# Convolution and GELU issued inside the second seven-product call of a feed-forward kernel

## The chip, the cores and the metric

The kernel runs on one NeuronCore of a Trainium2 chip. The metric is the device time of one execution in microseconds (us), as the median of several runs. The core's engines are TensorE (PE: matrix products; PEld is its weight loading), VectorE (DVE), ScalarE (ACT), GpSimd (POOL) and SyncE (SP, which here only starts DMAs). Each works through its own queue in order and waits for the others by semaphores.

## The reference

One layer of a decoder on 2048 prompt tokens and 64 sample tokens (8 sequences of 8), model width 1024, in float32: an attention mixer and a linear-attention mixer, an output projection, and a feed-forward block. The change touches the feed-forward block alone:

```
def conv_ffn(xn, conv_buf, w_up, conv_w, conv_b, w_down):
    up = xn @ w_up                                  # (T, 2 * 2816)
    g, u = jnp.split(up, 2, axis=-1)
    gp = jnp.concatenate([conv_buf, g], axis=1)     # two rows of the past in front
    c = conv_b + sum(conv_w[j] * gp[:, j:j + T] for j in range(3))
    h = jax.nn.gelu(c, approximate=False) * u
    return h @ w_down, gp[:, T:]
```

So the gate half `g` goes through a causal convolution of three taps along the tokens and a GELU, and is multiplied by the up half `u`; the product goes through the down projection.

## The kernel before, in words

The program runs the mixers first (up to about 1250 us of the profile), then the feed-forward block. Columns of the 2816-wide inner dimension lie on partitions (22 column tiles of 128), tokens along the free dimension. The 2112 tokens are cut into four chunks of 528 (two halves of H = 264). In a chunk the column tiles go in pairs, and the pairs in groups of 4, 4, 4, 4, 2 and 4 tiles, that is 2, 2, 2, 2, 1 and 2 pairs. Float32 products are made from three products of rounded parts (high times high, high times low, low times high), for which weights and inputs are split into a high part on ACT (line 70) and a low part on DVE (line 73).

For one pair of column tiles, `ffn` does this:

- the *gate call*: `strassen(c, f, 0, ...)` makes the gate columns of both tiles for both token halves, a 2 by 2 block product in seven products instead of eight. Each product is 12 matmuls of 128x128 by 264 columns (line 1628) into a PSUM bank: `pfa`, `pfb`, `pfa` again, `pfe`, `pfd`, `pfe` again, `pfd` again, numbered i = 0 to 6. Behind each product stands one evacuation: i = 0 copies to `p1` (ACT, line 1617), i = 1 adds the first result `o11` (DVE, line 1615), i = 2 copies to `u2` (ACT, line 1619), i = 3 makes the sum `u4`, i = 4 the result `o22`, i = 5 `o12` and i = 6 `o21` (all DVE, line 1615). The second use of `pfe` and of `pfd` adds to what is in the bank, so product 5 waits until `u4` has been read off and product 6 until `o22` has. `p1`, `u2` and `u4` have one buffer each. In the trace the results of a gate call are written to tiles `gt`, those of an up call to `up`.
- in the first pair of a group, the *down projection* of the group before (`down`, matmuls on line 92, sums on line 1656) is emitted between the gate call and what follows.
- for each tile j of the pair, the convolution: tap 2 and the bias in one ACT activation (line 1689), the copy of the last two rows to `halo` (DVE, line 1690), taps 1 and 0 as two DVE instructions (line 1698), and the GELU (ACT, line 1704). In the last chunk, which has the sample tokens, small copies (lines 1694 to 1696) and two small tap instructions (line 1702) are added.
- the *up call*: `strassen(c, f, 1, ...)`, as the gate call.
- for each tile the product of both (line 1708) and its split into `hh` and `hl` (lines 70 and 73), the input of the down projection.

Inside each `strassen` call the weights come from `wsrc`. In chunk 0 (and for the first two pairs also in chunk 1) four sums make the combined weights (lines 1594 to 1597) and all seven are split; for later chunks four of the seven are loaded ready-made from DRAM (`ws<-d_wst`), and three are split. A ring of 8 slots holds split weights (`ws`), one of 4 raw weights (`wr`). After each product the call also takes one step of other work: of `pend` (normalisation of another chunk) after even products, of `xp` (`xprep`, which prepares the inputs of the next chunk; its stores are started from ACT's queue) after odd ones.

Instructions are emitted in the order of the Python code. The order in which each engine runs them is made when the program is built: a scheduler with its own model of durations goes through time and gives each engine an instruction that it takes to be ready, an earlier emitted one before a later one. `self.after(b, a)` adds an order between two instructions without a semaphore. So a place in the code is a priority, and `after` is a fixed order. Products of neighbouring calls are mixed on PE in this way.

Of the kernel before, what the change touches and what calls it, by code (L numbers as in the profile page):

```python
# [10 lines left out]
F32 = mybir.dt.float32  # L11
F32R = mybir.dt.float32r
I32 = mybir.dt.int32
AF = mybir.ActivationFunctionType
ALU = mybir.AluOpType
# [12 lines left out]
H = 264  # L28
# [8 lines left out]
class Layer:  # L37
# [1569 lines left out]
            if c == cs and 2 <= i < 6:  # L1607
                nc.sync.dma_start(wt[i - 2], t.bitcast(F32))

    def strassen(self, c, f, z, xs, pend, xp, o11, o12, o21, o22):  # L1610
        nc = self.nc
        ws = self.wsrc(c, f, z)
        pa, pb, pd, pe = (self.bank(n) for n in ("pfa", "pfb", "pfd", "pfe"))
        p1, u2, u4 = (self.spool.tile([128, H], F32, name=self.n(n), tag=n, bufs=b) for n, b in (("p1", 1), ("u2", 1), ("u4", 1)))
        add = lambda o, x, y: nc.vector.tensor_tensor(o, x, y[:, :H], op=ALU.add)  # L1615
        for i, (bank, new, ev) in enumerate((
                (pa, True, lambda: nc.scalar.copy(p1, pa[:, :H])),
                (pb, True, lambda: add(o11, p1, pb)),
                (pa, False, lambda: nc.scalar.copy(u2, pa[:, :H])),
                (pe, True, lambda: add(u4, u2, pe)),  # L1620
                (pd, True, lambda: add(o22, u4, pd)),
                (pe, False, lambda: add(o12, u2, pe)),
                (pd, False, lambda: add(o21, u2, pd)))):
            w = next(ws)
            for k in range(4):
                xh, xl = xs[self.PROD[i]][k]
                for j, (ww, xx) in enumerate(((0, xh), (0, xl), (1, xh))):
                    self.lastmm = nc.tensor.matmul(bank[:, :H], w[:, ww, k, :], xx, start=new and k == 0 and j == 0,  # L1628
                                                   stop=k == 3 and j == 2, skip_group_check=not new)
            ev()  # L1630
            if i % 2 == 0:
                pend and next(pend, None)
            else:
                next(xp, None)
        next(ws, None)
# [7 lines left out]
    def down(self, c, gi, f0, G, hs, acc, last):  # L1643
        nc = self.nc
        for m in range(KT):
# [14 lines left out]
                self.ssq_add(self.fssq, acc[m], 2 * H, m == 0)  # L1660
            yield

    def ffn(self, c, xs, pend, more=None):
        nc, a, p, sp = self.nc, self.a, self.npool, self.spool
        halo, sc = self.halo, self.sc
        t0 = FCH[c][0]
        w = 2 * H
        npr = min(w, S - t0)
        acc = []
        f = 0  # L1670
        down = None
        xp = self.xprep(c + 1) if c < 3 else iter(())
        for gi, G in enumerate(FG):
            hs = []
            for pi in range(G // 2):
                gts = [self.ftile("gt", 3) for _ in range(2)]
                for j in range(2):
                    nc.vector.tensor_copy(gts[j][:, 0:2], halo[:, f + j, :])
                self.strassen(c, f, 0, xs, pend, xp if gi else iter(()), *(gts[j][:, 2 + z * H:2 + z * H + H] for j in range(2) for z in range(2)))
                if down is not None:  # L1680
                    for _ in down:
                        pass
                    down = None
                cts = []
                for j in range(2):
                    gt, ff = gts[j], f + j
                    ct = self.ftile("ct", 3)
                    cts.append(ct)
                    nc.scalar.activation(ct, gt[:, 2:], AF.Identity, bias=self.cw[:, ff, 3:4], scale=self.cw[:, ff, 2:3])
                    nc.vector.tensor_copy(halo[:, ff, :], gt[:, npr:npr + 2])  # L1690
                    gs = None
                    if npr < w:
                        gs = sp.tile([128, 8, 10], F32, name=self.n("gs"), tag="gs", bufs=2)
                        nc.vector.tensor_copy(gs[:, :, 0:2], sc[:, ff])
                        nc.vector.tensor_copy(gs[:, :, 2:10], gt[:, 2 + npr:].rearrange("p (b t) -> p b t", b=8))
                        nc.vector.tensor_copy(self.co[:, ff], gs[:, :, 8:10])
                    for tap in (1, 0):
                        nc.vector.scalar_tensor_tensor(ct[:, :npr], gt[:, tap:tap + npr], self.cw[:, ff, tap:tap + 1],
                                                       ct[:, :npr], op0=ALU.mult, op1=ALU.add)
                        if gs is not None:  # L1700
                            cs = ct[:, npr:w].rearrange("p (b t) -> p b t", b=8)
                            nc.vector.scalar_tensor_tensor(cs, gs[:, :, tap:tap + 8], self.cw[:, ff, tap:tap + 1],
                                                           cs, op0=ALU.mult, op1=ALU.add)
                    nc.scalar.activation(ct, ct, AF.Gelu)
                ups = [self.ftile("up", 2) for _ in range(2)]
                self.strassen(c, f, 1, xs, pend, xp if gi else iter(()), *(ups[j][:, z * H:z * H + H] for j in range(2) for z in range(2)))
                for j in range(2):
                    nc.vector.tensor_tensor(cts[j], cts[j], ups[j], op=ALU.mult)
                    hi = self.t528("hh", "hhl", 8, F32R)
                    lo = self.t528("hl", "hhl", 8, F32R)  # L1710
                    self.split(hi, lo, cts[j], "v")
                    hs.append((hi, lo))
                f += 2
            last = gi == len(FG) - 1
            if (last or gi == (c == 0)) and pend is not None:
                for _ in pend:
                    pass
                pend, more = more, None
            if not (last and c == 3):
                down = self.down(c, gi, f - G, G, hs, acc, last)  # L1720
        if c == 3:
            nc.sync.dma_start(a["o_cp"], halo)
            nc.sync.dma_start(a["o_cs"], self.co)
            return self.ffn_end(c, acc, hs, f - G, G)
        for _ in xp:
            pass
        for _ in self.xload(c + 1):
            pass
        for _ in down:
            pass  # L1730
        return self.final(c, acc, self.fssq, 0, w)
# [324 lines left out]
```

## Time and profile before

| | |
|---|---|
| time, median of 3 runs | 2740.87 us (2739.98 to 2741.07) |
| the profiled execution: time, span | 2739.73 us, 2737.9 us |
| PE, DVE, ACT, POOL busy | 97%, 67%, 46%, 14% of the span |
| feed-forward matmuls on line 1628, first and last start | 1252.1 us, 2697.2 us |
| the four taps' group (line 1698) | 176 instructions, median 759 ns |
| tap 2 with bias (line 1689), GELU (line 1704) | 88 of each, median 816 ns and 645 ns |
| first result of the up call (`up<-p,pfb`, line 1615) | 44 instructions, median 421 ns |

The profile is that of one execution. Times of a row count from the start of the span. An engine's busy time is the time in which one of its instructions ran; in a row of the timeline, brackets hold how long the engine had been idle before and which instruction released it. `pfd L92 <- ACT ws L70` reads: instructions on line 92 that write `pfd` waited for ACT's instruction on line 70 that writes `ws`.

### The profile page before, as it was taken

The page shows a single profiled execution, that of the slowest core. Times are in us where ns is not written, and L with a number is a line of the kernel's source. Part 1 is how long each engine was busy: PE and PEld are TensorE (multiplying, and loading weights), DVE is VectorE, ACT ScalarE, POOL GpSimd, SP SyncE. Part 2 cuts the span into 40 slices and gives each one's busy share as a digit, 9 for nine tenths or more (in the row PEclk, how much of TensorE's full clock was granted, in tenths as well). Part 3 has the DMA queues.
Part 4 walks back from the last instruction along what each step waited for, and adds up shares of the span by engine and source line. Part 5 has one row for each costly group of instructions (what it writes and reads, how often), then busy time and mean ns, then how long its engine had stood idle before and what let it go on. Part 6 is the DMA issues. An engine that isn't in the chain of part 4 may idle for free. (4 is left out here: it accounts for less than half of the span.)

```text
span 2737.9 us, 58183 instructions
## 1 busy us (share of the span) xinstructions
PE 2658.4 (97%) x22203; PEld 2518.3 (92%) x22203; DVE 1845.9 (67%) x4441; ACT 1271.2 (46%) x2961; POOL 386.4 (14%) x540
## 2 busy tenths in 40 slices
PE   8999999999999998999999999999999999999997
PEld 6788899888788888998999999999999999999997
DVE  7645655555467775568898889765676765766666
ACT  6535433333378784445554445433344432443332
POOL 2223120000035773011000020000110000200001
PEclk9999999999999999999999999999999999999998
DMA  8755546799776662476787588886798766976654
GB/s 322 250 176 178 183 149 196 283 331 365 267 262 181 200 168 93 154 264 230 259 281 275 191 330 306 329 305 201 246 335 287 280 227 215 327 248 215 216 193 147
DMA packets 287015, 661.66 MB, mean 242 GB/s; under 512 B 32961, under 2 KB 82753, under 8 KB 284689
## 3 DMA queue, kind: packets, MB, share of 16 engines
q1 hardware_dynamic: 256528, 579.53, 61.3%
q0 software_dynamic: 13216, 46.56, 5.0%
q10 hardware_dynamic: 16992, 31.86, 3.1%
q8 instruction: 175, 2.87, 0.4%
q14 instruction: 104, 0.84, 0.1%
HBM read 511.45 MB, written 146.37 MB: 240 GB/s over the span
## 5 line engine op out<-in xcount | busy, mean ns | idle before, releaser
L70 ACT ACTIVATE ws<-wr 128x512 fp32r<-128x512 f32 (+1 forms) x482 | 292.9, 616 | 426.8 <-PE pfe L1628 133.6
L92 PE MATMUL pfd<-hh,ws 128*128 128x264 f32 x2816 | 476.7, 286 | 6.0 <-ACT ws L70 4.5
L92 PEld LDWEIGHTS pfd<-hh,ws 128*128 128x128 f32 x2816 | 402.1, 190 | 8.6 <-ACT ws L70 6.4
L73 DVE TENSOR_TENSOR ws<-wr,ws 128x512 fp32r<-128x512 f32 (+1 forms) x482 | 319.2, 668 | 123.7 <-ACT ws L70 118.9
L92 PE MATMUL pfd<-hl,ws 128*128 128x264 f32 x1408 | 303.1, 286 | 1.9 <-DVE hl L73 1.9
L1628 PE MATMUL pfe<-xh,ws 128*128 128x264 f32 x1496 | 291.4, 287 | 11.4 <-DVE u L1615 6.9
L1628 PE MATMUL pfa<-xh,ws 128*128 128x264 f32 x1496 | 289.9, 285 | 4.6 <-ACT ws L70 2.2
L1628 PE MATMUL pfd<-xh,ws 128*128 128x264 f32 x1408 | 289.6, 285 | 1.9 <-DVE up L1615 1.4
L1628 PEld LDWEIGHTS pfe<-xh,ws 128*128 128x128 f32 x1496 | 237.4, 190 | 13.1 <-DVE u L1615 7.8
L1628 PEld LDWEIGHTS pfa<-xh,ws 128*128 128x128 f32 x1496 | 235.0, 188 | 6.1 <-ACT ws L70 2.8
L399 PE MATMUL pv<-wh,xh 128*128 128x256 f32 (+1 forms) x816 | 233.9, 287 | 2.2 <-DVE th L696 2.2
L1628 PEld LDWEIGHTS pfd<-xh,ws 128*128 128x128 f32 x1408 | 231.4, 189 | 2.9 <-DVE up L1615 1.8
L399 PE MATMUL pv<-wl,xh 128*128 128x256 f32 (+1 forms) x816 | 232.1, 284 | 0.0
L399 PE MATMUL pv<-wh,xl 128*128 128x256 f32 (+1 forms) x816 | 232.0, 284 | 0.0
L92 PEld LDWEIGHTS pfd<-hl,ws 128*128 128x128 f32 x1408 | 226.6, 190 | 2.2 <-DVE hl L73 2.1
L1869 ACT ACTIVATE ass<-ass,aml 128x256 f32<-128x256 f32 (+1 forms) x384 | 173.5, 454 | 62.6 <-DVE aml L1865 61.4
L1628 PE MATMUL pfd<-xl,ws 128*128 128x264 f32 x704 | 200.7, 285 | 0.5 <-DMA xl<-d_xst 0.5
L92 PE MATMUL pq<-xh,wh 128*128 128x512 f32 (+2 forms) x480 | 173.0, 366 | 8.3 <-ACT xh L234 7.9
L1656 DVE TENSOR_TENSOR acc<-acc,pfd 128x264 f32<-128x264 f32 x304 | 116.3, 422 | 89.6 <-PE pfd L92 89.1
L1628 PE MATMUL pfe<-xl,ws 128*128 128x264 f32 x616 | 176.3, 286 | 0.0
L1628 PE MATMUL pfa<-xl,ws 128*128 128x264 f32 x616 | 174.8, 284 | 0.0
L92 PE MATMUL pq<-xh,wl 128*128 128x512 f32 (+2 forms) x480 | 173.0, 361 | 0.0
(332 smaller groups left out, 6286.4 us busy)
## 6 DMA issues: line engine op xcount, KB each, us to landing
ws<-d_wst SPq DMA_DIRECT2D x248, 512.0 KB, 5.3
wr<-in_wu SPq DMA_DIRECT2D x114, 512.0 KB, 4.7
d_wst<-ws SPq DMA_DIRECT2D x88, 512.0 KB, 3.4
wr<-in_wd SPq DMA_DIRECT2D x160, 256.0 KB, 3.9
wr<-in_wt SPq DMA_DIRECT2D x60, 512.0 KB, 8.1
wh<-d_wbs SPq DMA_DIRECT2D x35, 512.0 KB, 5.7
wl<-d_wbs SPq DMA_DIRECT2D x35, 512.0 KB, 5.3
skp<-in_ckt SPq DMA_DIRECT2D x16, 1024.0 KB, 7.6
```

Source lines behind the costliest of these rows:

```text
L70: h = nc.scalar.activation(hi, src, AF.Copy)
L73: return h, (nc.gpsimd if lo_eng == "p" else nc.vector).tensor_tensor(lo, src, hi.bitcast(F32), op=ALU.subtract)
L92: mm = nc.tensor.matmul(o, ww[:, k, :], xx[:, s0:s0 + n], start=(k == order[0] and i == 0), stop=(k == order[-1] and i == 2))
L399: mm = nc.tensor.matmul(ps[:m, :256], x[:, t0:t0 + m], w[:, k % 4, :], start=(k == 0 and i == 0), stop=(k == KT - 1 and i == 2))
L1628: self.lastmm = nc.tensor.matmul(bank[:, :H], w[:, ww, k, :], xx, start=new and k == 0 and j == 0, stop=k == 3 and j == 2, skip_group_chec ...
L1656: nc.vector.tensor_tensor(acc[m][:, s0:s0 + n], acc[m][:, s0:s0 + n], pz, op=ALU.add)
L1869: ex = nc.scalar.activation(ssb[:, sc:sc + nk], ssb[:, sc:sc + nk], AF.Exp, bias=self.ml[:, idx, h:h + 1], scale=-1.0, accum_out=self.ml[: ...
```

## The change

`strassen` takes a generator `mid` and goes one step of it on after each of its products; it also keeps each evacuation instruction in `self.lev[i]`. The convolution of a pair, which was emitted in front of the up call, becomes a generator `conv` that the up call is given as `mid`. Its five steps fall behind products 0 to 4 of the up call: tile 0's tap 2, bias and halo copy; tile 0's taps 1 and 0; tile 1's tap 2, bias and halo copy; tile 1's taps 1 and 0; both GELUs. In addition `after` orders tile 0's taps behind the up call's `o11` sum, tile 1's taps behind its `u4` sum (both on DVE), and both GELUs behind its `u2` copy (ACT). Both `ct` tiles of a pair are allocated before the call. No instruction is added or taken out.

```
-    def strassen(self, c, f, z, xs, pend, xp, o11, o12, o21, o22):
+    def strassen(self, c, f, z, xs, pend, xp, o11, o12, o21, o22, mid=None):
...
-            ev()
+            self.lev[i] = ev()
+            mid and next(mid, None)
             if i % 2 == 0:
                 pend and next(pend, None)
...
+    lev = {}
+
+    def conv(self, f, npr, gts, cts):
+        nc, w, halo = self.nc, 2 * H, self.halo
+        for j in range(2):
+            gt, ct, ff = gts[j], cts[j], f + j
+            nc.scalar.activation(ct, gt[:, 2:], AF.Identity, bias=self.cw[:, ff, 3:4], scale=self.cw[:, ff, 2:3])
+            nc.vector.tensor_copy(halo[:, ff, :], gt[:, npr:npr + 2])
...
+            yield
+            for tap in (1, 0):
+                st = nc.vector.scalar_tensor_tensor(ct[:, :npr], gt[:, tap:tap + npr], self.cw[:, ff, tap:tap + 1],
+                                               ct[:, :npr], op0=ALU.mult, op1=ALU.add)
+                self.after(st, self.lev[2 * j + 1])
...
+            yield
+        for ct in cts:
+            self.after(nc.scalar.activation(ct, ct, AF.Gelu), self.lev[2])
+        yield
...
-                cts = []
-                for j in range(2):
...
-                    nc.scalar.activation(ct, ct, AF.Gelu)
+                cts = [self.ftile("ct", 3) for _ in range(2)]
+                mid = self.conv(f, npr, gts, cts)
                 ups = [self.ftile("up", 2) for _ in range(2)]
-                self.strassen(c, f, 1, xs, pend, xp if gi else iter(()), *(ups[j][:, z * H:z * H + H] for j in range(2) for z in range(2)))
+                self.strassen(c, f, 1, xs, pend, xp if gi else iter(()), *(ups[j][:, z * H:z * H + H] for j in range(2) for z in range(2)), mid=mid)
+                for _ in mid:
+                    pass
```

More of the change, by code (lines that the diff above doesn't have):

```diff
@@ L1661, in down @@
             yield
+    lev = {}
[5 more added lines that the diff above has]
+            nc.vector.tensor_copy(halo[:, ff, :], gt[:, npr:npr + 2])
+            gs = None
+            if npr < w:
+                gs = self.spool.tile([128, 8, 10], F32, name=self.n("gs"), tag="gs", bufs=2)
+                nc.vector.tensor_copy(gs[:, :, 0:2], self.sc[:, ff])
+                nc.vector.tensor_copy(gs[:, :, 2:10], gt[:, 2 + npr:].rearrange("p (b t) -> p b t", b=8))
+                nc.vector.tensor_copy(self.co[:, ff], gs[:, :, 8:10])
+            yield
[3 more added lines that the diff above has]
+                self.after(st, self.lev[2 * j + 1])
+                if gs is not None:
+                    cs = ct[:, npr:w].rearrange("p (b t) -> p b t", b=8)
+                    nc.vector.scalar_tensor_tensor(cs, gs[:, :, tap:tap + 8], self.cw[:, ff, tap:tap + 1],
+                                                   cs, op0=ALU.mult, op1=ALU.add)
+            yield
+        for ct in cts:
+            self.after(nc.scalar.activation(ct, ct, AF.Gelu), self.lev[2])
+        yield
     def ffn(self, c, xs, pend, more=None):
@@ L1683, in ffn @@
                     down = None
-                cts = []
-                for j in range(2):
[L1686 to L1704, printed above, removed]
+                cts = [self.ftile("ct", 3) for _ in range(2)]
+                mid = self.conv(f, npr, gts, cts)
                 ups = [self.ftile("up", 2) for _ in range(2)]
-                self.strassen(c, f, 1, xs, pend, xp if gi else iter(()), *(ups[j][:, z * H:z * H + H] for j in range(2) for z in range(2)))
+                self.strassen(c, f, 1, xs, pend, xp if gi else iter(()), *(ups[j][:, z * H:z * H + H] for j in range(2) for z in range(2)), mid=mid)
+                for _ in mid:
+                    pass
                 for j in range(2):
```

## The prediction

> **What bounds the kernel now.** I read the page first (busy shares), then the feed-forward stage by chunk, then what the matrix engine (PE) waits for in each chunk, then the instructions around the largest wait in order of time.
>
> ```profile
> span 2737.9 us, 58183 instructions
> PE 2658.4 (97%) x22203; PEld 2518.3 (92%) x22203; DVE 1845.9 (67%) x4441; ACT 1271.2 (46%) x2961; POOL 386.4 (14%) x540
> ```
>
> PE is busy 97% of the span, so a change of work on DVE (VectorE) or ACT (ScalarE) can pay only where PE waits. The next view cuts the feed-forward stage into its four token chunks: columns are the length of the stretch, busy time of each engine (with its count of instructions), granted clock, DMA share and GB/s.
>
> ```profile
> core 0: us, PE busy (x) PEld busy (x) DVE busy (x) ACT busy (x) POOL busy (x), PEclk, DMA share, GB/s
> 1252.00:1630.00 378.00, 363.59 (x2924) 360.17 (x2924) 328.89 (x660) 196.00 (x360) 21.05 (x37) 0.99 0.71 255
> 1630.00:2002.00 372.00, 362.50 (x2937) 360.44 (x2936) 271.15 (x555) 154.33 (x288) 18.78 (x30) 0.99 0.80 282
> 2002.00:2359.00 357.00, 355.73 (x2919) 355.06 (x2918) 239.73 (x498) 141.29 (x264) 16.52 (x29) 1.00 0.77 271
> 2359.00:2700.00 341.00, 339.95 (x2783) 338.92 (x2781) 218.99 (x541) 128.28 (x240) 1.20 (x1) 1.00 0.69 231
> ```
>
> Chunks 2 and 3 leave PE idle 1.3 and 1.1 us in 357 and 341 us: nothing is to be had there, only lost. Chunk 0 leaves 14.4 us and chunk 1 leaves 9.5 us, and in chunk 0 DVE is busy 329 of 378 us. So the change is decided in chunks 0 and 1. What PE waited for there (us in total, times, longest), from the waits of chunk 0, then of chunk 1, then of chunks 2 and 3:
>
> ```profile
> PE pfe L1628 <- DVE u L1615: 6.9, 3, 5.6
> PE pfd L92 <- ACT ws L70: 3.4, 3, 2.0
> ...
> PE pfe L1628 <- DMA ws<-d_wst: 3.9, 3, 1.5
> PE pfd L92 <- DVE hl L73: 1.9, 1, 1.9
> PE pfa L1628 <- ACT ws L70: 1.2, 1, 1.2
> ...
> PE pfa L1628 <- ACT p L1617: 1.0, 2, 0.5
> ```
>
> The largest is one wait of 5.6 us for the sum `u4` (tile `u`). Around it, in order of time (start, duration, engine, line, out<-in, and in brackets the idle time before it): PE, then DVE, then ACT, then the stretch right behind the wait.
>
> ```profile
> 1271.79 0.28 PE L1628 MATMUL pfd<-xh,ws 128*128 128x264 f32 x1
> 1277.71 0.59 PE L1628 MATMUL pfe<-xh,ws 128*128 128x264 f32 x1 [5.64 <-DVE u L1615]
> ...
> 1270.58 0.76 DVE L1698 SCALAR_TENSOR_TENSOR ct<-gt,c_cw,ct 128x528 f32<-128x528 f32 x1
> 1271.25 0.68 DVE L1597 TENSOR_TENSOR wt<-wr,wt 128x512 f32<-128x512 f32 x1
> ...
> 1274.34 0.42 DVE L1615 TENSOR_TENSOR gt<-u,pfd 128x264 f32<-128x264 f32 x1
> ...
> 1275.95 0.68 DVE L1595 TENSOR_TENSOR wr<-wr 128x512 f32<-128x512 f32 x1
> 1276.56 0.76 DVE L1698 SCALAR_TENSOR_TENSOR ct<-gt,c_cw,ct 128x528 f32<-128x528 f32 x1
> 1277.23 0.42 DVE L1615 TENSOR_TENSOR u<-u,pfe 128x264 f32<-128x264 f32 x1
> ...
> 1274.79 0.83 ACT L1689 ACTIVATE ct<-gt,c_cw 128x528 f32<-128x528 f32 x1
> 1275.53 0.36 ACT L1619 COPY u<-pfa 128x264 f32<-128x264 f32 x1
> ...
> 1277.70:1282.20 4.50, 4.49 (x20) 4.50 (x21) 3.67 (x8) 1.52 (x3) 0.00 (x0) 0.50 0.07 27
> ```
>
> The tile `u2` has one buffer, so the copy `u2` (1275.53) of the up call could not be written before the gate call's last sum `gt<-u,pfd` (1274.34) had read the old one. ACT then did the tap-2 activation (L1689) first, because it is emitted earlier and was freed by the same sum; DVE did a weight sum and one tap (1276.56) before `u4`. PE lost 5.64 us, and then 4.5 us at a granted clock of 0.50, which costs 2.2 us more.
>
> **The change, part by part.** *No work is added or removed.* Per pair the moved step issues two L1689 activations, two halo copies, four taps (L1698; in chunk 3 also six small copies and four small taps) and two GELUs: all on DVE and ACT, no DMA, nothing on POOL or SP. It is moved behind the up call's weight loads on SP and behind the steps of the post chain and of `xprep` only in the order of emission; SP's queue holds none of its instructions. The work itself is therefore 0 us; what counts is place.
>
> *The pins.* Taps of tile 0 now stand on DVE behind the up call's first sum (`up<-p,pfb`), taps of tile 1 behind `u4`, GELUs on ACT behind `u2`. They are orders on one engine, so they add no semaphore; what queues behind a waiting tap is the next sums and the low halves of the weight splits, and behind a waiting GELU the high halves. That such waits happen is in the waits of ACT:
>
> ```profile
> ACT ct L1704 <- DVE ct L1698: 47.3, 34, 3.9
> ```
>
> That is 34 waits of a GELU for its tap; in chunks 2 and 3 they can have cost PE no more than the 1 us above. GELUs can't become late for their reader (L1708), which needs the call's last sum.
>
> *Gain 1: the 5.64 us wait.* `u2` is now emitted ahead of tile 1's L1689: it saves that activation's slot, 1275.53 - 1274.79 = 0.74 us. The tap at 1276.56 can't stand ahead of `u4` any more: 1277.23 - 1276.56 = 0.67 us, of which the weight sum at 1275.95 keeps a little. I take 1.3 us together. The two taps of tile 0 (one of them at 1270.58) may stay where they are, as their pin is already met, and so may the weight sums; hence `gt<-u,pfd` stays near 1274.34 and some 4.3 us of the wait stay, with the half clock behind it. Next late is the sum after `u4`. Bounds: 0, and the whole 5.6 + 2.2 = 7.8 us if the new order on DVE serves `gt<-u,pfd` at once.
>
> *Gain 2: second pair of chunk 1.* Rows of ACT, then PE, then the stretch behind them:
>
> ```profile
> 1671.65 0.83 ACT L1689 ACTIVATE ct<-gt,c_cw 128x528 f32<-128x528 f32 x1 [0.84 <-DVE gt L1615]
> ...
> 1673.05 0.39 PE L1628 MATMUL pfa<-xh,ws 128*128 128x264 f32 x1 [1.25 <-ACT ws L70]
> 1675.94 0.52 PE L1628 MATMUL pfa<-xh,ws 128*128 128x264 f32 x2 [0.94 <-DVE ws L73]
> ...
> 1678.50:1681.30 2.80, 2.78 (x12) 2.78 (x13) 2.49 (x7) 0.96 (x4) 0.00 (x0) 0.50 1.05 406
> ```
>
> The L1689 activation waited 0.84 us at the head of ACT's queue with a weight split behind it, and PE waited 1.25 us for that split. Emitted behind the up call's first product, it no longer stands ahead of that product's split. Bounds 0 and 1.25 + 0.94 = 2.2 us; I take the middle, 1.1 us. The last row shows a clock of 0.50 for 2.8 us behind these gaps, none of them longer than 1.25 us in the rows; so a half clock can outlive a long wait that is broken into short ones, and I count no gain for it here.
>
> On this the Trainium skill, "TensorE: Matmul & The Clock Gate", section "HAM oscillation — how this bites in real kernels", has the rule "no PE-idle gaps >~3.4µs". By that rule the 2.2 us behind the first wait would go as soon as less than 3.4 us of it were left; the row at 1678.50 does not agree that a single gap must be so long. With some 4.3 us left, both leave it in place.
>
> *Loss: the taps leave the down projection.* In every group but a chunk's first, the down projection of the group before runs between the first pair's gate and up calls. DVE used it for that pair's taps. First and last of the four taps of chunk 0's third pair, the sum behind which they must now stand, then the stretches by time: the down projection, and the five stretches from such an up call to the next down projection or group.
>
> ```profile
> 1320.22 0.76 DVE L1698 SCALAR_TENSOR_TENSOR ct<-gt,c_cw,ct 128x528 f32<-128x528 f32 x1
> ...
> 1325.94 0.76 DVE L1698 SCALAR_TENSOR_TENSOR ct<-gt,c_cw,ct 128x528 f32<-128x528 f32 x1
> ...
> 1345.58 0.41 DVE L1615 TENSOR_TENSOR up<-p,pfb 128x264 f32<-128x264 f32 x1
> ...
> 1313.00:1341.00 28.00, 28.00 (x231) 28.00 (x231) 19.25 (x37) 15.69 (x37) 0.00 (x0) 1.00 0.62 220
> 1341.00:1378.00 37.00, 36.39 (x296) 35.97 (x295) 35.05 (x69) 20.63 (x39) 0.00 (x0) 1.00 0.85 315
> ...
> 1406.00:1448.00 42.00, 38.63 (x309) 37.58 (x307) 39.03 (x78) 21.83 (x41) 0.00 (x0) 1.00 0.91 328
> ...
> 1476.00:1515.00 39.00, 39.00 (x322) 39.00 (x322) 34.39 (x68) 21.40 (x39) 0.00 (x0) 1.00 0.77 275
> ...
> 1542.00:1577.00 35.00, 35.00 (x290) 35.00 (x289) 27.55 (x61) 17.62 (x35) 0.00 (x0) 1.00 0.50 177
> 1577.00:1612.00 35.00, 33.26 (x268) 32.48 (x267) 30.75 (x63) 17.13 (x32) 9.68 (x18) 1.00 0.96 347
> ```
>
> The taps go some 20 us later, out of a stretch with 8.75 us of idle DVE into one with 1.95 us. A tap takes 0.67 us of DVE's queue (1270.58 to 1271.25), four take 2.7 us. The five stretches have 1.95, 2.97, 4.6, 7.5 and 4.3 us free. The first is short by 0.75 us; in the second PE already waits 3.4 us, so I charge half of the 2.7 us, 1.35; the others fit. Loss 2.1 us; bounds 0 and five times 2.7 = 13.6 us. In chunks 2 and 3 the same move finds room: in the up call of such a pair (chunk 3) DVE was idle ahead of `u4` and of the next split for
>
> ```profile
> 2443.90 0.43 DVE L1615 TENSOR_TENSOR u<-u,pfe 128x264 f32<-128x264 f32 x1 [2.81 <-ACT u L1619]
> ...
> 2447.40 0.69 DVE L73 TENSOR_TENSOR ws<-wr,ws 128x512 fp32r<-128x512 f32 x1 [2.01 <-ACT ws L70]
> ```
>
> 2.81 and 2.01 us, against 1.4 us of taps at each place (2.0 with chunk 3's small ones): 0. If that cover were gone, the ten such pairs of chunks 2 and 3 would pay up to 2.7 us each.
>
> *Sum.* -1.3 - 1.1 + 2.1 = -0.3 us. The profiled execution took 2739.73 us, of which the span is 2737.9; that is 1.1 us under the median of 2740.87. -0.3 on the median gives 2740.6 us. A measurement of this kernel tells some 0.2%, 5.5 us, from no change.
>
> **The rivals.** *B, the first wait goes whole.* For it: 2.3 us of DVE's queue stood between the end of PE's last product (1271.79 + 0.28 = 1272.07) and `gt<-u,pfd` at 1274.34, and moved priorities may dissolve it. Against it: most are weight work, which the move does not put later. It gives -7.8 - 1.1 and no loss: 2740.9 - 8.9 = 2732 us, or 2734 if the half clock outlives the wait. (The Trainium skill's rule on the clock gate, above, would have the first of these, the row at 1678.50 allows the second.)
>
> *C, slower: the pile in chunk 0.* Taps pinned behind `u4` stand ahead of the sum that frees the bank for the seventh product; where DVE is later than one product, PE stops. For it: 35.05 of 37 us busy, and PE waits already in two of the five stretches. Against it: free DVE in three of them. It decides once taps cost more than the free time: 2.7 us in the first two stretches and half of it in three is 9.5 us, less the 2.4 gained: 2748 us. All five in full: 2752.
>
> *D, nothing moves that PE sees.* Both gains and the loss are hidden behind fillers from the next call: 2740.9, inside the forecast.
>
> **How the numbers follow.** Forecast with D (gain and loss of like size): 0.52, its own range 2736 to 2745. B and lesser forms of it beyond 5.5 us: 0.26. C: 0.22. The range goes from 2731, just under B, to 2750, above C's 2748, and leaves out the full pile. So faster 0.26, same 0.52, slower 0.22.
>
> **What would show it.** Right: the wait for `u` in chunk 0 is 4 to 5 us with clock 0.50 behind it; PE idle in chunks 2 and 3 stays near 1 us; DVE idle in 1313 to 1341 grows by 2.7 us and shrinks after 1341. Wrong: the 5.6 us wait gone (B), new PE waits for `up` or `ws` after 1341 (C), or new waits in chunks 2 and 3, for which I have charged nothing.

## The result and the profile after

The change made the kernel faster: 2726.28 us (median of four runs, 2723.55 to 2730.01) against 2740.76 us, ratio 0.9947 [0.9933, 0.9961]. Repeated beside twelve runs of the kernel before it gave 2726.73 against 2736.69 us, ratio 0.9968 [0.9957, 0.9980]. In the later comparisons the kernel before had medians of 2735.4 to 2736.8 us over 116 runs (2730.3 to 2747.3), so the first four of it were among its slower ones, and I take the effect as some 10 us. In microseconds below, differences are differences of medians of runs made together.

The page after, of a run of 2730.01 us, 9.7 us less than the profiled run before; then the four chunks as in the prediction (length, PE busy, PEld, DVE, ACT, POOL, granted clock, DMA share, GB/s):

```profile
span 2728.2 us, 58216 instructions
PE 2657.1 (97%) x22203; PEld 2519.3 (92%) x22203; DVE 1852.7 (68%) x4441; ACT 1270.3 (47%) x2961; POOL 385.0 (14%) x540
```

```profile
1254.00:1629.00 375.00, 361.89 (x2924) 358.57 (x2924) 328.75 (x660) 196.89 (x360) 21.60 (x38) 0.99 0.72 256
1629.00:1992.00 363.00, 359.35 (x2937) 357.67 (x2937) 271.84 (x554) 153.46 (x288) 18.18 (x30) 1.00 0.82 291
1992.00:2352.00 360.00, 357.33 (x2922) 356.90 (x2921) 241.15 (x498) 141.06 (x264) 16.51 (x29) 1.00 0.77 268
2352.00:2690.00 338.00, 337.53 (x2771) 337.32 (x2770) 223.81 (x541) 127.35 (x240) 1.20 (x1) 1.00 0.68 233
```

The work is the same (x4441 on DVE, x2961 on ACT before and after). PE idle went from 14.4 to 13.1 us in chunk 0, from 9.5 to 3.7 in chunk 1, from 1.3 to 2.7 in chunk 2 and from 1.1 to 0.5 in chunk 3. That is 6.3 us. Time at half clock counts as busy: by the traces' clock records it cost PE 7.1 us before, in four stretches (near 1278, 1450, 1679 and 1696), and 4.0 us after, in two (near 1279 and 2171), which is 3.1 us less. By the starts of the chunks' first products in the trace (for chunk 3, to the start of its last product) the four took 378.2, 372.0, 357.3 and 337.6 us before and 375.3, 362.8, 359.9 and 335.3 us after. Together that is 11.7 us less, of which idle time and half clock are 9.4; the span gained only 9.7, as the first product started 2.0 us later.

The waits of PE after, in the order of the prediction (total, times, longest): chunk 0, chunk 1, chunks 2 and 3.

```profile
PE pfe L1628 <- DVE u L1615: 5.2, 3, 4.8
PE pfd L92 <- ACT ws L70: 3.2, 4, 1.2
PE pfa L1628 <- ACT ws L70: 2.8, 4, 1.0
...
PE pfe L1628 <- DMA ws<-d_wst: 0.9, 2, 0.5
PE pfa L1628 <- ACT ws L70: 0.7, 1, 0.7
...
PE pfa L1628 <- ACT p L1617: 3.1, 3, 2.2
```

The large wait of chunk 0 is still there, a little shorter. In chunk 1 the wait for `hl` (1.9 us) is gone. Chunk 2 has a new wait of 2.2 us for the copy `p`, with a half clock behind it. Around the large wait (PE, ACT, DVE, then the stretch behind it; in the changed kernel taps are L1680, the tap-2 activation L1670, the GELU L1689):

```profile
1278.84 0.59 PE L1628 MATMUL pfe<-xh,ws 128*128 128x264 f32 x1 [4.81 <-DVE u L1615]
...
1276.60 0.38 ACT L1619 COPY u<-pfa 128x264 f32<-128x264 f32 x1 [1.91 <-DVE gt L1615]
1276.88 0.83 ACT L1670 ACTIVATE ct<-gt,c_cw 128x528 f32<-128x528 f32 x1
...
1274.27 0.76 DVE L1680 SCALAR_TENSOR_TENSOR ct<-gt,c_cw,ct 128x528 f32<-128x528 f32 x1
...
1276.15 0.42 DVE L1615 TENSOR_TENSOR gt<-u,pfd 128x264 f32<-128x264 f32 x1
1278.37 0.41 DVE L1615 TENSOR_TENSOR u<-u,pfe 128x264 f32<-128x264 f32 x1
...
1278.90:1283.40 4.50, 4.50 (x20) 4.50 (x21) 4.28 (x9) 2.27 (x5) 0.00 (x0) 0.50 0.20 80
```

The copy `u2` now stands ahead of tile 1's tap-2 activation. But the sum `gt<-u,pfd`, for which it waits, is as late as before: taps of tile 0 and weight sums still stand in front of it. The half clock behind the wait stayed. What went is seen in chunk 1, where the prediction's second gain lies. Before, a third wait followed the two near 1673 and 1676 that the prediction shows (first row); after, two short ones are left:

```profile
1678.52 0.59 PE L1628 MATMUL pfe<-xh,ws 128*128 128x264 f32 x1 [1.10 <-DMA ws<-d_wst]
...
1670.69 0.39 PE L1628 MATMUL pfa<-xh,ws 128*128 128x264 f32 x1 [0.72 <-ACT ws L70]
1673.27 0.52 PE L1628 MATMUL pfa<-xh,ws 128*128 128x264 f32 x2 [0.62 <-DVE ws L73]
```

Three waits of 3.3 us in all became 1.3 us, and the half clock there (1.7 us) went with them: the granted clock was 1.00 from 1670 to 1685.

### The profile page after: what moved, and what is told of

It is laid out like the page before. It is cut to its first block, busy times and chain, and to the rows that moved or that the text cites. A ratio compares the mean times of both kernels' runs of the same rounds, so it can differ in the third digit from the quotient of the medians.

```text
span 2728.2 us, 58216 instructions
## 1 busy us (share of the span) xinstructions
PE 2657.1 (97%) x22203; PEld 2519.3 (92%) x22203; DVE 1852.7 (68%) x4441; ACT 1270.3 (47%) x2961; POOL 385.0 (14%) x540
## 4 chain that ended last, share of the span: by engine, by line
PE 77%; DMA 8%; DVE 7%; POOL 3%; issue 3%; ACT 2%; SPq 0%; DVEq 0%; POOLq 0%; ACTq 0%
PE pfd L92 16%; PE pv L399 9%; PE pfe L1628 8%; PE pfd L1628 8%; PE pq L92 8%; PE pfa L1628 8%; PE pbo L1431 7%; PE pfb L1628 4%; PE pas L1872 2%; DMA raw<-in_xn 2%; DVE ws L73 2%; PE pao L1915 1%; POOL aop L1229 1%; PE pat L1898 1%; DMA wr<-in_wd 1%
```

## Where the gain is: experiments

All of them change only the order of the same work, unless said. "Old place" is the code before, in front of the up call. One more reading rule: chunk 0 in its unchanged form took 374.6 to 378.2 us in five profiles. Chunk 1 took 371.4 to 372.7 us in three, and 367.4 us in `only_c0`, where its code is unchanged too. So a chunk of a single profile can say little below 4 to 5 us; the medians decide.

**Orders or emission.** `nopins` takes the three explicit orders out.

```diff
-                self.after(st, self.lev[2 * j + 1])
-            self.after(nc.scalar.activation(ct, ct, AF.Gelu), self.lev[2])
+            nc.scalar.activation(ct, ct, AF.Gelu)
```

> Whole move, but without the three fixed orders (taps behind the up call's sums, GELUs behind u2); only the place of emission changes. Theory P (priority: the up call's weight splits and sums are now emitted ahead of the convolution, and that is what pays): as the changed kernel, 2723 to 2730 us. Theory F (the fixed orders pay, because without them the scheduler still fills idle DVE with taps as in the kernel before): 2736 to 2741 us, and the taps of a group's first pair stay in the down projection, some 20 us ahead of up<-p,pfb.

2725.99 against 2735.77 us, 0.9957 [0.9942, 0.9972]: 9.8 us faster, as much as the change. The place in the order of emission pays; the orders aren't needed for the gain.

**By chunk.** `only_c0`, `only_c1`, `only_c23`: the step moved in some chunks only.

```diff
+                if c == 0:        # c == 1; c > 1
...                               # new place
+                else:
...                               # old place
```

> The change in chunk 0 alone, chunks 1 to 3 as before. By the profiles of before and after, chunk 0 is 2.9 us shorter. Theory L (each chunk's gain is local, the sum of the waits removed in it): 2737 to 2738.5 us. Theory R (rival: chunk 0's new order hands DVE and the DMAs to chunk 1 in a better state, and chunk 1's gain of 9 us comes from there): 2728 to 2732 us.

> The change in chunk 1 alone. Chunk 1 is 9.1 us shorter in the profile after. Theory L (local): 2730 to 2733 us, with PE's waits for ws<-d_wst and hl in chunk 1 gone as in the profile after. Theory R (the gain of chunk 1 is handed over by chunk 0): 2737 to 2741 us.

> The change in chunks 2 and 3 alone. In the profile after, chunk 2 is 2.5 us longer with one wait of 2.2 us for p<-pfa behind a late load, chunk 3 is 2.3 us shorter. Theory L with that wait in every run: 2740 to 2742 us. Theory L with the wait in some runs only (a late load, which would be why the runs of the changed kernel spread over 6.5 us): a spread of several us, median 2736 to 2740 us. My prediction's step (nothing moves in chunks 2 and 3): 2740 to 2742 us and a spread of 1 us.

Against 2735.77 us: 2733.77, 0.9984 [0.9974, 0.9993]; 2734.77, 0.9993 [0.9984, 1.0002]; 2734.32, 0.9992 [0.9981, 1.0003]. That is -2.0, -1.0 and -1.5 us by medians and -4.4, -1.9 and -2.2 us by the ratios: 4.5 us by the first count, 8.5 by the second, and the last two intervals include no change. So whether the parts add up to the whole isn't settled; no chunk holds the gain alone. Of the two theories on chunk 1, that its gain is its own and that chunk 0 hands it over, neither got its 9 us. In the trace chunk 1 was 367.4 us with only chunk 0 changed, 368.5 with only itself changed and 362.8 in the change.

**By pair.** `only_first` and `only_second`: the step moved only in the first pair of each group (between whose calls the down projection of the group before runs), or only in the second.

```diff
+                if pi == 0:       # pi == 1
...                               # new place
+                else:
...                               # old place
```

> The move made for the first pair of each group alone (24 of 44 pairs); in these the down projection of the group before runs between gate and up call, and the taps leave it. My prediction's loss term: 2 us slower than before, chunk 0 longer by 2 us with new waits in the up call behind the down projection. Theory P (place in the order pays wherever it is changed, and the taps find room): 3 to 7 us faster, no chunk longer by more than 1 us.

> The move made for the second pair of each group alone (20 of 44 pairs), where the up call follows the gate call directly. My prediction's split of gains: the wait for u in the first pair of chunk 0 stays as it was, only the waits near 1673 and 1676 in chunk 1 shrink: 1 to 2 us faster. Theory P: 3 to 7 us faster, as many as the first pairs bring. If the gains of chunk 1 come from hl of the second pair of its first group (its split no longer behind a loading operation): chunk 1 shorter by 4 us or more, chunk 0 within 1 us.

First pairs: 2740.82 against 2736.56 us, 1.0014 [1.0005, 1.0023], 4.3 us slower. Second pairs: 2725.71 us, 0.9962 [0.9950, 0.9974], 10.9 us faster, more than any of the expectations. This is the cut that separates gain from loss. Chunk 0 took 381.8 us with first pairs and 371.7 with second pairs moved; the wait for `u` near 1277 stayed in both (5.0 and 5.6 us). Part of what the second pairs gain in chunk 0 is seen near 1440, in the up call of the second pair of the third group and the next gate call. Before (PE's waits, then ACT, DVE, a stretch):

```profile
1445.42 0.39 PE L1628 MATMUL pfd<-xh,ws 128*128 128x264 f32 x1 [0.97 <-DVE up L1615]
1449.15 0.61 PE L92 MATMUL pfd<-hh,ws 128*128 128x264 f32 x2 [2.01 <-ACT ws L70]
...
1437.59 0.35 ACT L1619 COPY u<-pfa 128x264 f32<-128x264 f32 x1
...
1439.46 0.75 DVE L1698 SCALAR_TENSOR_TENSOR ct<-gt,c_cw,ct 128x528 f32<-128x528 f32 x1
1441.10 0.41 DVE L1615 TENSOR_TENSOR u<-u,pfe 128x264 f32<-128x264 f32 x1
...
1450.00:1451.00 1.00, 1.00 (x6) 1.00 (x6) 1.00 (x3) 0.00 (x0) 0.00 (x0) 0.50 0.99 326
```

`only_second`, the same rows:

```profile
1445.77 0.51 PE L92 MATMUL pfd<-hh,ws 128*128 128x264 f32 x2 [0.72 <-ACT ws L70]
...
1436.22 0.35 ACT L1619 COPY u<-pfa 128x264 f32<-128x264 f32 x1
...
1436.30 0.76 DVE L1680 SCALAR_TENSOR_TENSOR ct<-gt,c_cw,ct 128x528 f32<-128x528 f32 x1
1437.58 0.42 DVE L1615 TENSOR_TENSOR u<-u,pfe 128x264 f32<-128x264 f32 x1
...
1450.00:1451.00 1.00, 1.00 (x10) 1.00 (x10) 1.00 (x3) 0.00 (x0) 0.00 (x0) 1.00 1.00 344
```

Before, `u4` ended its wait in DVE's queue 1441.10 - 1437.94 = 3.2 us after `u2` was copied, behind two taps (1438.17 and 1439.46); with the move it starts 1.0 us after it, behind one. The waits of 0.97 and 2.01 us behind it are gone or down to 0.72, and so is the half clock (6 products in a microsecond instead of 10; 1.7 us in all, one minus the granted clock summed over 1449 to 1453). The whole change shows the same: `u2` at 1439.43, `u4` at 1441.55 and no half clock. So do the others: of the eleven kernels that move chunk 0's second pairs, none has a PE wait over 1.0 us from 1440 to 1460; of the other nine, seven have one, of 1.65 to 3.06 us (not `only_first` and `u2_in_p1`).

**Activation or taps.** `gelu_only` moves only the two GELUs (tap-2 activation, halo and taps at the old place, all pairs); `second_act` moves, in second pairs, taps and GELUs with their orders and leaves the two tap-2 activations and halo copies at the old place.

```diff
 # gelu_only: all steps but the last are run in front of the up call
+                for _ in range(4):
+                    next(mid)
 # second_act: one step with both activations and halos, run in front of the call
+                    next(mid)
```

> Only the two GELUs of a pair are issued inside the up call (behind its fifth product); the tap-2 activations, halo copies and taps stand in front of the call as in the kernel before; no explicit orders. Theory A (ScalarE's queue: a GELU that waits for its taps holds up the splits and copies of the up call): the greater part of the whole move's gain, 6 to 12 us faster than before. Theory V (VectorE's queue: taps stand ahead of the up call's sums): within 2 us of before, the 5.6 us wait for u in chunk 0 unchanged. If both count: 3 to 6 us faster.

> Second pairs of each group only: the two tap-2 activations and the halo copies stand in front of the up call as in the kernel before; taps and GELUs are steps inside it, with the orders of the change. (The whole step moved in second pairs alone: 10.9 us faster than before.) Theory U (the copy u2 of the up call stands behind tile 1's tap-2 activation on ScalarE, as at 1436.87 and 1437.59 in chunk 0, and u4 and the products behind it come late): most of the gain is lost, 0 to 4 us faster than before. Theory V (on VectorE the taps stand ahead of the up call's sums, as the two at 1438.17 and 1439.46 ahead of u4): most of it stays, 7 to 11 us faster.

`gelu_only`: 2738.50 against 2736.56 us, 1.0005 [0.9996, 1.0014]: no gain, the wait for `u` 5.4 us. `second_act`: 2726.80 against 2735.41 us, 0.9965 [0.9951, 0.9978]: 8.6 us faster, nearly all of the second pairs' gain. So it is the place of the taps on DVE that pays (with the GELUs that must follow them), and neither ACT's tap-2 activation ahead of `u2` nor the place of the GELUs alone.

**What the orders do.** `second_nopins` and `first_nopins`: as the two cuts by pair, without orders.

```diff
-                self.after(st, self.lev[2 * j + 1])
-            self.after(nc.scalar.activation(ct, ct, AF.Gelu), self.lev[2])
+            nc.scalar.activation(ct, ct, AF.Gelu)
```

> Second pairs of each group only, without the explicit orders. If the place in the order of emission alone pays: 9 to 12 us faster than before, as with the orders. If the order behind the up call's sums is what keeps the taps from standing ahead of them: at most 6 us faster, with taps again ahead of u4 in chunk 0 near 1437.

> First pairs of each group only, without the explicit orders of taps and GELUs (with them: 4.3 us slower than before, chunk 0 longer by 3.6 us). Theory O (the orders cost it: taps held behind sums of the up call that run at the same time as the down projection's end): the loss goes, within 2 us of before, chunk 0 at 376 to 378 us. Theory D (the taps lose the down projection as their time, wherever they stand after it, the loss term of my prediction): it stays, 3 to 5 us slower than before.

Against 2735.41 us: second pairs 2727.29, 0.9969 [0.9957, 0.9981]; first pairs 2736.80, 1.0001 [0.9989, 1.0013]. Second pairs gain with orders or without. First pairs lose 4.3 us with them and nothing that can be told without; the two intervals overlap, so by these runs alone the difference isn't clear of noise. Nor does `first_nopins` show that taps may leave the down projection for nothing, since there they do not leave it. The third pair of chunk 0, its last tap and the up call's first sum in `first_nopins`, then the sum and the first tap in `only_first`:

```profile
1327.93 0.76 DVE L1680 SCALAR_TENSOR_TENSOR ct<-gt,c_cw,ct 128x528 f32<-128x528 f32 x1
1347.34 0.42 DVE L1615 TENSOR_TENSOR up<-p,pfb 128x264 f32<-128x264 f32 x1
...
1343.08 0.42 DVE L1615 TENSOR_TENSOR up<-p,pfb 128x264 f32<-128x264 f32 x1
1343.42 0.76 DVE L1680 SCALAR_TENSOR_TENSOR ct<-gt,c_cw,ct 128x528 f32<-128x528 f32 x1
```

Without orders the scheduler still places these taps in the down projection, 19.4 us ahead of that sum (19.6 before), though they are emitted later. This holds for all 20 pairs that have a down projection between their calls: their last taps stand 6 to 20 us ahead of the sum, as before. Only the orders drive the taps out of it. So the loss came where the taps left the down projection, as the prediction had it; whether the lost room there or the order behind the sums costs it, no run separates. It also explains `nopins`: behind down projections its taps stand where they stood before, so it is in effect the move of the second pairs. The same is true of `pins_second` and `u2_pins_second` below. In chunk 0 the waits of `only_first` are spread over the starts of down projections and products:

```profile
PE pfd L92 <- ACT ws L70: 4.4, 4, 1.6
PE pfa L1628 <- ACT ws L70: 2.5, 4, 0.7
PE pfd L92 <- DVE up L1615: 2.1, 3, 1.4
```

They were 3.4, 0.9 and 0.8 us before.

**Chunk 1's wait for `hl`.** Before, an operation of `post_late` (the normalisation of chunk 3, one of the `pend` steps) that waited for its load stood on DVE ahead of the second pair's `hl`, for which PE waited; a half clock followed (DVE, PE, stretch):

```profile
1693.12 0.77 DVE L1506 SCALAR_TENSOR_TENSOR bo<-bo,c_gvec,brb 128x528 f32<-128x528 f32 x1 [2.15 <-DMA bo<-d_x]
1694.42 0.70 DVE L73 TENSOR_TENSOR hl<-ct,hh 128x528 fp32r<-128x528 f32 x1
...
1695.18 0.81 PE L92 MATMUL pfd<-hl,ws 128*128 128x264 f32 x2 [1.92 <-DVE hl L73]
...
1696.00:1697.00 1.00, 1.00 (x6) 1.00 (x6) 1.00 (x3) 0.28 (x1) 0.00 (x0) 0.50 0.82 315
```

`bo_step` puts an empty step between that load and its operation; `bo_pin` orders the operation behind the last product emitted. Both leave convolution and GELU as they were.

```diff
 # bo_step
             yield
+            yield
 # bo_pin
-            nc.vector.scalar_tensor_tensor(o, o, self.gv[:, 1, m:m + 1], rb, ...)
+            self.after(nc.vector.scalar_tensor_tensor(o, o, self.gv[:, 1, m:m + 1], rb, ...), self.lastmm)
```

> The kernel before with one more empty step in post_late between a tile's loads and the vector operations that use them; convolution and GELU untouched, same work. In the kernel before, PE waits 1.9 us for hl near 1695 (third gap cluster of chunk 1, followed by a half clock of about 2.4 us) and the operation ahead of hl on DVE had waited 2.15 us for its load of bo. Theory S (a large part of chunk 1's gain is only that the moved steps put this loading operation elsewhere in DVE's queue): the wait for hl and its half clock go, chunk 1 gets 3 to 4.5 us shorter, the whole 3 to 5 us shorter than before, without touching the convolution. Theory Q (the queue of the convolution itself is what PE waits for, the load is incidental): the wait for hl stays above 1 us or moves to the next tile; the whole within 1.5 us of before.

> The kernel before with one order more: post_late's first operation of a tile (bo) on VectorE waits for the last product emitted before it; convolution and GELU untouched. In VectorE's order the second such operation now stands behind both hl splits of chunk 1's first group and not in front of them. Theory S (in chunk 1 part of the gain is that this operation, waiting for its load, no longer stands ahead of hl): PE's 1.9 us wait for hl near 1695 goes, and with it the half clock of some 2.4 us, chunk 1 3 to 4.5 us shorter, the whole 2.5 to 5 us faster. Theory K (the half clock and the gap come back with the next late operation, since VectorE has the same work to do): the wait for hl goes, but chunk 1 within 1.5 us of before.

`bo_step` tells nothing on the cause: 2737.64 against 2736.56 us, 0.9996 [0.9988, 1.0005], and the operation kept its place ahead of `hl` and its wait (2.55 us). `bo_pin` moved it behind both `hl`, and PE's wait there went:

```profile
1694.12 0.70 DVE L73 TENSOR_TENSOR hl<-ct,hh 128x528 fp32r<-128x528 f32 x1
1695.89 0.76 DVE L1506 SCALAR_TENSOR_TENSOR bo<-bo,c_gvec,brb 128x528 f32<-128x528 f32 x1
...
1694.07 0.99 PE L92 MATMUL pfd<-hh,ws 128*128 128x264 f32 x6 [0.28 <-ACT hh L70]
```

Chunk 1 was 367.3 us in its profile instead of 372.0, but the whole gave 2735.63 against 2736.78 us, 0.9991 [0.9982, 1.0001]: 1.1 us. The mechanism of that wait is shown; what it is worth is not: the 4.7 us of the one profile are not borne out by the median, and the interval goes from 4.9 us faster to no change. So at most 5 us of the change's gain is this.

**The buffer of `u2`.** `u2_in_p1` is the kernel before with `u2` written into `p1`'s tile, which gets two buffers; the room that they take is the same.

```diff
-        p1, u2, u4 = (... (("p1", 1), ("u2", 1), ("u4", 1)))
+        p1, u4 = (... (("p1", 2), ("u4", 1)))
+        u2 = p1
```

> The kernel before with one thing changed: p1 gets two buffers and u2 is written into p1's tile (p1 is dead by then), so that the copy u2 of a call need not wait until the last sum of the call before has read the old u2; convolution and GELU untouched. Theory U1 (the single buffer of u2 is the root of the 5.64 us wait in chunk 0): that wait falls below 2.5 us and the half clock behind it goes, chunk 0 shorter by 4 to 8 us, the whole 4 to 9 us faster. Theory Z (ScalarE's and VectorE's queues hold u2 and u4 up in any case, by the GELU with its table load, the tap-2 activation and the taps): the wait stays above 4 us, the whole within 2 us of before.

2725.37 against 2735.41 us, 0.9959 [0.9943, 0.9975]: 10.0 us faster, with the convolution at its old place. (Lines are one higher here; the copy `u2` appears as p<-pfa, L1620. PE, ACT, DVE, stretch.)

```profile
1270.61 0.39 PE L1629 MATMUL pfe<-xh,ws 128*128 128x264 f32 x1 [1.12 <-DVE u L1616]
1273.86 0.36 PE L1629 MATMUL pfd<-xh,ws 128*128 128x264 f32 x1 [1.53 <-DVE up L1616]
...
1268.37 0.38 ACT L1620 COPY p<-pfa 128x264 f32<-128x264 f32 x1 [0.32 <-DVE up L1616]
...
1270.14 0.42 DVE L1616 TENSOR_TENSOR u<-p,pfe 128x264 f32<-128x264 f32 x1
1272.36 0.42 DVE L1616 TENSOR_TENSOR gt<-p,pfd 128x264 f32<-128x264 f32 x1
...
1270.00:1274.00 4.00, 1.86 (x13) 1.68 (x14) 4.00 (x9) 3.62 (x5) 0.00 (x0) 1.00 0.00 0
```

`u2` and `u4` now come before the gate call's last sum (1272.36), not after it. The 5.64 us wait became 1.12 and 1.53 us, and the clock stayed at 1.00. That is the root of the wait on which my first gain rested: neither an activation nor a tap, but one buffer. Its gain isn't in this wait alone: in the profile, of a run 4.9 us under the median, chunk 0 was 7.1 us shorter than before and chunk 1 8.2 us.

**Together.** `u2_second`: second pairs with orders and `u2` in `p1`. `pins_second`: all pairs, orders in second pairs alone. `u2_pins_second`: that and `u2`. `u2_after`: the whole change and `u2`. `after_again`: the change itself.

```diff
 # pins_second, u2_pins_second
+                if self.pin:                 # pi == 1
+                    self.after(st, self.lev[2 * j + 1])
```

> The move in second pairs alone with its orders (10.9 us faster than before by itself) and u2 written into p1's tile with two buffers (10.0 us faster by itself). If both take the same waits away (gt<-u,pfd releases u2, and taps stood in front of that sum): together 10 to 13 us faster, chunk 0 near 370 us. If they are different waits: 16 to 21 us faster, chunk 0 at 366 us or less.

> The change with its orders kept in second pairs alone; the step is moved in all pairs. If the orders in first pairs are the loss (first pairs with orders +4.3 us, without 1.4): 9 to 11 us faster than before, chunk 0 near 371 us instead of 375 us as in the change. If the whole change is as good as its second pairs in any case: chunk 0 stays near 375 us, and the time is that of the change.

> The step moved in all pairs, orders in second pairs alone, and u2 in p1's tile. Candidate for the fastest: if first pairs without orders cost or bring nothing, as u2_second within 2 us; if moving them helps once u2 no longer waits for the sum of the call before, 2 to 4 us faster than u2_second.

> The change itself once more, beside more runs of the kernel before. First result: 14.5 us faster, against four runs of before with a median of 2740.8; in the later runs of before the median was 2735.4 to 2736.8. Parts: second pairs alone 10.9 us faster, first pairs alone 4.3 us slower. If the parts add: 6 to 8 us faster. If the first pairs' loss is lost in the whole: 9 to 12 us faster. If the first result was the size: 13 to 16 us faster.

> The whole change (all pairs, all orders) with u2 in p1's tile, against u2_second (the same without the first pairs, 17.2 us faster than before). If the orders in first pairs cost 4 us: 12 to 14 us faster. If they cost nothing beside moved second pairs: 16 to 18 us faster.

| kernel | us | before, same runs | ratio |
|---|---|---|---|
| `u2_second` | 2719.58 | 2736.78 | 0.9935 [0.9922, 0.9948] |
| `u2_pins_second` | 2719.69 | 2736.78 | 0.9935 [0.9923, 0.9948] |
| `pins_second` | 2729.04 | 2736.78 | 0.9962 [0.9949, 0.9976] |
| `u2_after` | 2724.39 | 2736.69 | 0.9955 [0.9943, 0.9967] |
| `after_again` | 2726.73 | 2736.69 | 0.9968 [0.9957, 0.9980] |

The buffer and the second pairs mostly take different waits away: 17.2 us together, against 10.0 and 10.9 alone. `u2_second` and `u2_pins_second` are the fastest versions found, and beat the change by some 7 us. The first two chunks of `u2_second`, with chunk 0 not down to the 366 us that I had expected of different waits:

```profile
1252.00:1624.00 372.00, 362.57 (x2929) 359.94 (x2929) 330.66 (x666) 195.01 (x360) 24.85 (x38) 0.99 0.71 260
1624.00:1987.00 363.00, 359.15 (x2937) 357.57 (x2936) 268.65 (x551) 154.18 (x288) 18.73 (x30) 1.00 0.80 289
```

`u2_after` and `u2_pins_second` differ in the orders of first pairs alone, with which the taps leave the down projection: 12.3 against 17.1 us, so these orders cost 4.8 us once `u2` is free, about as much as by themselves. In the change itself they can't be told: it is 10.0 us faster, its second pairs alone 10.9, and `pins_second` 7.7. The sum of both parts, 10.9 - 4.3 = 6.6 us, lies inside the change's interval of 5.5 to 11.8 us, so the loss may be there unseen or may be smaller there; that wasn't settled.

## Why the prediction was wrong, point by point

**What bounds the kernel:** right. The time came from chunks 0 and 1; chunks 2 and 3 changed by +2.6 and -2.3 us in the profile, and their move alone gave 1.5 us by the median, which is not clear of no change.

**Gain 1:** right that most of the wait would stay. 4.81 us were left of 5.64 (I had said 4.3), and the half clock stayed at 0.50, as the step and the rule of the Trainium skill beside it had it. The size is not shown: the wait was 4.81 to 5.24 us in the four profiles with this pair moved as in the change (`after`, `after_again`, `only_c0`, `only_first`) and 4.97 to 5.94 us in `before` and seven others that leave it, so the gain is nearer half a microsecond than 1.3. I had named `u2`'s one buffer and still priced only the convolution's instructions behind it; the wait hangs on that buffer.

**Gain 2:** mis-sized. I priced it at the two waits near 1673 and 1676 and left all other second pairs at nothing. In that place itself the profile of the change shows 3.7 us (the waits and their half clock), above my bound of 2.2, though `only_c1` has a wait of 4.31 us there. In chunk 0 the same pairs cost PE 0.97 and 2.01 us and 1.7 us of half clock near 1445 to 1453. I had quoted that stretch (1406 to 1448, PE idle 3.4 us), and used it only as a place where taps would pile up. It was where taps already stood in the way. Second pairs brought 10.9 us [7 to 14 by the interval] where the term was 1.1 with a bound of 2.2: this is the step that failed.

**Loss:** by itself real and larger than I took it, 4.3 us against 2.1, within the bounds, and seen only in kernels in which the taps left the down projection. I had counted two of the five stretches as having PE waits; by their rows three have (0.6, 3.4 and 1.7 us idle). DVE's busy time in 1313 to 1341 fell from 19.25 to 16.71 us, 2.5 us, as predicted (2.7). But the first stretch that I charged lost only 0.8 us of PE (36.39 busy before, 35.56 after), and chunk 0 got shorter, not longer; moved alone, its second pairs gained more than its first pairs lost.

**Half clock counted at nothing:** wrong as a rule of the sum. I took it from the stretch at 1678.50, but in the change the half clock went there, near 1450 and near 1697, with 1.7 us each. A new one came in chunk 2 (1.7 us).

**Rivals:** none took place. B had the faster side with the wrong mechanism (the first wait did not go). C's pile did not come in full: PE's waits for `ws` at `pfa` in chunk 0 grew from 0.9 to 2.8 us, but the chunk got shorter. D would have left the waits of chunk 1. One sign that I had named as wrong did come: the wait of 2.2 us in chunk 2 (2.6 us in `after_again`), for which I had charged nothing. The base did its part too: 2740.87 us was the median of three runs, and 116 later ones lie some 4 us lower.

## What to carry to other kernels

Where DVE is full, a PE wait in a stretch that I expect to fill up further is first of all evidence of what stands in that queue now: price every wait of such a stretch as a gain of the move before pricing it as a loss. Cut a reordering by the position of its instances (here first and second pairs of a group), since gain and loss lay in different ones. Look in the trace whether the moved instructions moved: a place in the emission is only a priority, and in 20 pairs it moved no tap. Before reordering around a wait, follow it to the buffer that it hangs on: one more buffer brought as much as the whole move, and with the second pairs' move 17.2 us.

## What the runs showed of the hardware

A single wait of about 2 us can be followed by a half clock, but need not be. In the kernel before, 1.92 us at 1695.18 and 2.01 us at 1449.15 were each followed by a granted clock of 0.50 (rows above), and in `u2_in_p1` so was the first of these; the second, a longer wait in `only_c0`, was not:

```profile
1600.84 1.63 PE L92 MATMUL pfd<-hh,ws 128*128 128x264 f32 x8 [2.21 <-ACT hh L70]
...
1602.00:1603.00 1.00, 1.00 (x7) 1.00 (x6) 0.78 (x2) 0.18 (x1) 0.48 (x1) 0.50 1.00 386
...
1676.45 0.39 PE L1628 MATMUL pfe<-xh,ws 128*128 128x264 f32 x1 [2.99 <-DMA ws<-d_wst]
...
1677.00:1678.00 1.00, 1.00 (x10) 1.00 (x9) 1.00 (x3) 0.00 (x0) 0.00 (x0) 1.00 0.98 382
```

The waits of 1.12 and 1.53 us in `u2_in_p1` and of 2.64 us near 2169 in `after_again` were not followed by one either. What decides between such waits, no run here shows. By the clock records of the 20 traces each half clock in the feed-forward block lasted 3.41 us (29 times), 6.83 us (14 times) or 10.24 us (once); one of 3.41 us costs 1.7 us where PE is busy throughout. The Trainium skill, "TensorE: Matmul & The Clock Gate", section "HAM oscillation — how this bites in real kernels", sets the limit at gaps over some 3.4 us; the waits of 1.92, 2.01 and 2.21 us do not agree.

And the kernel's time spreads more than its first runs told: 2730.3 to 2747.3 us in 116 runs of the same kernel before, with 2739.98 to 2741.07 in the first. The 116 came from five comparisons on five chips, with medians within 1.4 us of each other; on which chip the first were made is not on record.
